# A hybrid conformer / mLSTM block on one core: heads' output turned on VectorE, tokens loaded first, start pinned, transposes mid-step, FFN entry rearranged

## The chip, the core and the metric

One of the eight cores of a Trainium2 chip. The time is that of one execution on the device, in microseconds (us); of a kernel's runs the median is given. The engines have their own instruction queues, which run in the order written: TensorE (PE: products, transposes, always into PSUM), VectorE (DVE), ScalarE (ACT), GpSimd (POOL) and SyncE (SP, which here only issues DMAs; POOL issues some too). An instruction waits at the head of its queue until the semaphores that it names have come, and all behind it wait with it.

## The reference

One layer of a diffusion backbone over 512 latent tokens (`x`, width 1024) and 256 context tokens (`ctx`), in float32:

```python
h  = rmsnorm(x) * (1 + sc1(c)) + sh1(c)          # ctx likewise, from c_ctx
p  = h @ w_in                                    # parts: glu, q, k, v, p5, gates, ab
A  = silu(layernorm(dwconv31(p0 * sigmoid(p1)))) @ w_conv_out
hm = mLSTM(q, k, v, gates)                       # 4 heads of 512, both directions
B  = (rmsnorm_per_head(hm) * m_norm_g * sigmoid(p5)) @ w_m_out
y  = sigmoid(p7) * A + sigmoid(p8) * B
x  = x + ga1 * (y @ w_out)
x  = x + ga2 * (relu((rmsnorm(x)*(1+sc2)+sh2) @ w1)**2 @ w2)
out = rmsnorm(x) * final_g
```

The six vectors sh1 ... ga2 are products of silu(c) with a 1024 x 6144 matrix and a bias.

## The kernel before, in words

Nearly every matrix product is made of three, of a rounded high part and a remainder: a weight tile `wraw` (128 x 1024) is loaded by SP, ACT casts it to `whi` (L99), DVE takes the rest as `wlo` (L100), and `mm3` (L103) multiplies hi x hi, hi x lo, lo x hi. So each weight tile costs one DMA, one ACT and one DVE instruction. `split` (L108) does the same for activations. Buffers come from pools: three of `wraw`, four each of `whi` and `wlo`, and the PSUM banks in two groups of four ("a", "b"). The order on each engine is set by a scheduler from the program's order, priorities and buffers; `issue_after` ties one instruction behind another.

Stages, with the times of the profiled execution:

- **Start (0 to 63 us).** The row c is spread over the partitions by a product and put through silu (`crow`, cL). `modload` (L189) loads the two wm tiles of one 128-channel step j, `moddot` (L197) multiplies them with cL and sums along the row, on DVE; small operations add the bias. Four token tiles xt are loaded; `xnorm` (L181) squares them on ACT with a running sum, takes 1/sqrt on POOL (`rstd_`) and scales the tile on DVE (L185). For each of eight steps j, `hmake` (L208) transposes the four tiles' 128 columns on PE (pt), applies scale and shift on ACT (hf) and splits into hT; six products of three (sacc, 18 matmuls) follow.
- **Gates (125 to 165 us).** 64 rows of gate logits go through scans on DVE; `finish` (L300) transposes Z on PE into the bank pz, and DVE copies it to zm (L305). The bank is used again by the products of p5, shown as p.
- **Heads (to 790 us).** Per head: k and q tiles with a 5-tap convolution, scores, four blocks of weights, v, and then per token tile t eighteen products into po. ACT sums the squares of po, POOL takes 1/sqrt, DVE makes hm (L555). `store` (L538), one tile late, makes four PE transposes into th, four ACT scalings with the norm's gain into st (L544, one buffer), and one DMA to hd (L546) in runs of 128 tokens (512 bytes). A 31-tap convolution (ca, L372) fills DVE at low priority. `lnfinish` (L397) stores mean and 1/sigma of the LayerNorm to lnd.
- **Branches (to 970 us).** The statistics are loaded back (lnr), normalised branch tiles and the heads' output (`hmload`, L692: load, cast, split) are multiplied with w_conv_out and w_m_out (pym). 32 more modulation tiles wmt come over POOL's queue, two ahead, and `mod` (L649) takes one dot at a time on DVE.
- **Output projection to FFN (970 to 1019 us).** The last three eighths of y @ w_out are done tile by tile (`last_part`, L788); then per token tile the residual add on DVE (L797), squares on ACT (L799), 1/sqrt on POOL, scale and shift on DVE (xh, L808 and L810), eight transposes on PE (pt), cast and split into h2T. `ff1(0)` runs in two halves of 256 tokens, `row` (L704) turns ga2 into a row on all partitions: PE transpose, ACT copy, DMA out (rowd), DMA back.
- **FFN (to the end).** Eight groups: `ff1`, `w2load` (scales w2 by ga2 on DVE, L862, casts, splits), `ff2`.

## Time and profile before

| | |
|---|---|
| median of 3 runs | 1356.4 us (1356.16 to 1357.19) |
| the profiled execution | 1357.05 us, span 1355.3, mean granted clock 0.995 |
| PE busy | 1324.4 us (98%), 6266 matmuls |
| DVE / ACT / POOL busy | 936.7 / 602.5 / 68.9 us |
| DMA | 176.36 MB in 65205 packets, 6594 of them under 512 bytes |

PE is busy nearly all the time, so the table's 98% says little of where time can be won; the list of what PE waited for and the windows by stage do. Matmuls are pipelined: the recorded length of one (0.39 us for 512 columns) is longer than the distance between the starts of two, which is the time that one more of them costs.

### The profile page before, as it was taken

The numbers are of one execution on the slowest core, as the hardware profiler recorded it, in microseconds if no ns is written. First come the engines' busy times: TensorE is split into PE (matmuls) and PEld (weight loads), VectorE is DVE, ScalarE is ACT, GpSimd is POOL, SyncE is SP. The second block draws the span as 40 slices with busy tenths as digits, with TensorE's granted clock in tenths as the row PEclk, the third lists the DMA queues.
The fourth block names the chain that finished last, engine by engine and source line by source line (L and its number), as shares of the span: only waits on it lengthen the run. The fifth ranks groups of instructions, "written<-read, shape, count | busy, mean of one in ns | idle before, by whom it ended". The sixth has DMA issues, their size and how long they took to land.

```text
span 1355.3 us, 16676 instructions
## 1 busy us (share of the span) xinstructions
PE 1324.4 (98%) x6266; PEld 1104.1 (81%) x6266; DVE 936.7 (69%) x1457; ACT 602.5 (44%) x912; POOL 68.9 (5%) x231
## 2 busy tenths in 40 slices
PE   5999999999999999999999999999999999999997
PEld 3788788888888888888888878888798888888885
DVE  5789978489674896748995477766684454554535
ACT  4548664346533465344635274322354323342223
POOL 2000100000000000000000000100000000000001
PEclk9999999999999999999999999999989999999999
DMA  9793233223332233322334479765633322333202
GB/s 329 288 334 110 89 112 105 62 63 101 104 94 67 64 100 107 96 63 66 106 96 127 124 249 312 262 189 200 219 106 96 97 92 63 123 109 109 73 22 78
DMA packets 65205, 176.36 MB, mean 130 GB/s; under 512 B 6594, under 2 KB 19042, under 8 KB 65124
## 3 DMA queue, kind: packets, MB, share of 16 engines
q1 hardware_dynamic: 60516, 158.51, 36.0%
q0 software_dynamic: 4608, 16.78, 3.9%
q8 instruction: 49, 0.80, 0.2%
q14 instruction: 32, 0.26, 0.1%
HBM read 162.99 MB, written 12.27 MB: 129 GB/s over the span
## 4 chain that ended last, share of the span: by engine, by line
PE 88%; DVE 4%; ACT 2%; DMA 2%; issue 1%; POOL 1%; SPq 0%; POOLq 0%; ACTq 0%; DVEq 0%
PE pf L104 8%; PE pf L105 8%; PE pf L106 8%; PE pv L105 3%; PE pv L104 3%; PE pv L106 3%; PE pym L106 2%; PE pym L105 2%; PE pym L104 2%; PE p L104 2%; PE p L106 2%; PE p L105 2%; PE pq L106 2%; PE pq L104 2%; PE pq L105 2%; PE pg L104 2%
## 5 line engine op out<-in xcount | busy, mean ns | idle before, releaser
L99 ACT CAST whi<-wraw 128x1024 fp32r<-128x1024 f32 (+1 forms) x159 | 164.9, 1040 | 305.7 <-PE pv L106 74.6
L100 DVE TENSOR_TENSOR wlo<-wraw,whi 128x1024 fp32r<-128x1024 f32 (+1 forms) x159 | 191.6, 1206 | 87.9 <-ACT whi L99 87.4
L372 DVE SCALAR_TENSOR_TENSOR ca<-up,col,ca 128x512 f32<-128x512 f32 x240 | 179.5, 748 | 5.7 <-ACT ca L370 0.9
L332 DVE SCALAR_TENSOR_TENSOR cacc<-craw,col,cacc 128x512 f32<-128x512 f32 (+1 forms) x128 | 110.7, 876 | 0.0
L864 ACT CAST w2h<-w2raw 128x1024 fp32r<-128x1024 f32 x32 | 32.3, 1052 | 156.3 <-PE pf L106 124.8
L105 PE MATMUL pf<-w2l,fT 128*128 128x512 f32 x256 | 99.6, 390 | 0.0
L104 PE MATMUL pf<-w2h,fT 128*128 128x512 f32 x256 | 99.2, 390 | 0.2 <-ACT w2h L864 0.2
L106 PE MATMUL pf<-w2h,fT 128*128 128x512 f32 x256 | 99.5, 389 | 0.0
L884 DVE TENSOR_TENSOR x<-pf,x 128x512 f32<-128x512 f32 x64 | 44.0, 689 | 65.8 <-PE pf L106 65.7
L104 PE MATMUL pf<-h2T,whi 128*128 128x512 f32 x224 | 87.1, 389 | 0.0
L105 PE MATMUL pf<-h2T,whi 128*128 128x512 f32 x224 | 87.1, 389 | 0.0
L106 PE MATMUL pf<-h2T,wlo 128*128 128x512 f32 x224 | 87.1, 389 | 0.0
L104 PE MATMUL pv<-whi,hT 128*128 128x512 f32 x192 | 75.4, 393 | 0.0
L106 PE MATMUL pv<-whi,hT 128*128 128x512 f32 x192 | 74.7, 389 | 0.0
L105 PE MATMUL pv<-wlo,hT 128*128 128x512 f32 x192 | 74.7, 389 | 0.0
L862 DVE TENSOR_TENSOR w2raw<-w2raw,ga 128x1024 f32<-128x1024 f32 x32 | 39.2, 1225 | 47.5 <-DMA w2raw<-in_w 46.4
L104 PEld LDWEIGHTS pf<-w2h,fT 128*128 128x128 f32 x256 | 48.0, 188 | 10.7 <-ACT w2h L864 0.7
L105 PEld LDWEIGHTS pf<-w2l,fT 128*128 128x128 f32 x256 | 48.1, 188 | 10.6 <-DVE w2l L869 0.7
L106 PEld LDWEIGHTS pf<-w2h,fT 128*128 128x128 f32 x256 | 48.1, 188 | 9.8
L104 PE MATMUL p<-whi,hT 128*128 128x512 f32 x128 | 50.8, 397 | 2.2 <-DVE zm L305 2.2
L869 DVE TENSOR_TENSOR w2l<-w2raw,w2h 128x512 fp32r<-128x512 f32 x64 | 40.7, 686 | 15.0 <-ACT w2h L864 15.0
L104 PE MATMUL pg<-hT,whi 128*128 128x512 f32 x128 | 50.6, 395 | 0.0
(354 smaller groups left out, 3344.1 us busy)
## 6 DMA issues: line engine op xcount, KB each, us to landing
wm<-in_wmt SPq DMA_DIRECT2D x32, 512.0 KB, 6.0
wmt<-in_wmt POOLq DMA_DIRECT2D x32, 512.0 KB, 4.7
wraw<-in_wqk SPq DMA_DIRECT2D x32, 512.0 KB, 3.5
wraw<-in_w SPq DMA_DIRECT2D x32, 512.0 KB, 4.7
w2raw<-in_w SPq DMA_DIRECT2D x32, 512.0 KB, 3.6
wraw<-in_wglu SPq DMA_DIRECT2D x16, 512.0 KB, 3.8
wraw<-in_wp SPq DMA_DIRECT2D x16, 512.0 KB, 3.6
wraw<-in_wv SPq DMA_DIRECT2D x16, 512.0 KB, 3.5
```

Source lines behind the costliest of these rows:

```text
L99: nc.scalar.copy(out=hi[:, s], in_=raw[:, s])
L100: wlast[0] = nc.vector.tensor_tensor(out=lo[:, s], in0=raw[:, s], in1=hi[:, s].bitcast(F32), op=ALU.subtract)
L104: mm(dst, lhsT=l[0], rhs=r[0], start=start, stop=False)
L105: mm(dst, lhsT=l[0], rhs=r[1], start=False, stop=False)
L106: mm(dst, lhsT=l[1], rhs=r[0], start=False, stop=stop)
L332: nc.vector.scalar_tensor_tensor(out=acc[:, :n], in0=raw[:, d:d + n], scalar=ccol(wc + d), in1=acc[:, :n], op0=ALU.mult, op1=ALU.add)
L372: nc.vector.scalar_tensor_tensor(out=accv, in0=up[:, :, d:d + 64], scalar=w_, in1=accv, op0=ALU.mult, op1=ALU.add)
L862: nc.vector.tensor_tensor(out=raw, in0=raw, in1=ga2, op=ALU.mult)
L864: nc.scalar.copy(out=hi, in_=raw)
L869: nc.vector.tensor_tensor(out=l_, in0=raw[:, nn], in1=hi[:, nn].bitcast(F32), op=ALU.subtract)
L884: nc.vector.tensor_tensor(out=x1[t][:, nn], in0=pf, in1=x1[t][:, nn], op=ALU.add)
```

## The change

1. **Start.** The four xt tiles are loaded ahead of col and the wm tiles. Squares of tiles 1 and 3 go to DVE. DVE scales only the first 384 columns of each tile up front; ACT scales the other 640 during step 0. Squares, scalings, dots and splits up to step 1 are tied into a fixed order on ACT, DVE and PE (`pin`). Weights, modulation and transposes of step j+1 are issued inside step j, the transposes between its two halves of products.
2. **zm** is copied from its bank by ACT instead of DVE.
3. **LayerNorm statistics** stay in two on-chip tiles (lns); the round trip through lnd goes.
4. **Heads' output.** `store` runs at once, not a tile late: DVE transposes hm in blocks of 32 x 32 into st, and four DMAs put the blocks in place, in runs of 32 tokens (128 bytes). The gain is applied in `hmload`.
5. **Output projection to FFN.** The remaining modulation dots move behind the h2T splits (`mod(tlast[0])` in `w1load`). Squares are written into the used PSUM bank. Scaling, transposing and casting of a tile (`scaled`, `turned`) are issued in a written order: tile 0 is turned ahead of the last tile's products, tile 1 behind them, tiles 2 and 3 ahead of the second half of `ff1(0)` (`rest`).
6. **ga2** is made into a row behind the last product of `ff1(0)`, not ahead of its first.

The diff, cut:

```diff
+        def pin(e, f):
+            if e in pins:
+                with tc.issue_after(pins[e].ins):
+                    pins[e] = f()
+            else:
+                pins[e] = f()
+            return pins[e]
...
-            nc.vector.tensor_scalar(out=xt, in0=xt, scalar1=rs[:, t:t + 1], scalar2=None, op0=ALU.mult)
+        def xscale(t, xt, n):
+            return nc.vector.tensor_scalar(out=xt[:, :n], in0=xt[:, :n], scalar1=rs[:, t:t + 1], scalar2=None,
+                                           op0=ALU.mult)
...
-        raw0 = modload(0, (1,))
+            hi, lo = hT[j][:, 0, o:o + n], hT[j][:, 1, o:o + n]
+            p("act", lambda: nc.scalar.activation(out=hf[:, :n], in_=pt[:, :n], func=AF.Identity,
+                                                  scale=m1[:, c, j, 1:2], bias=m1[:, c, j, 0:1]))
+            p("act", lambda: nc.scalar.copy(out=hi, in_=hf[:, :n]))
+            p("dve", lambda: nc.vector.tensor_tensor(out=lo, in0=hf[:, :n], in1=hi.bitcast(F32), op=ALU.subtract))
         xl = [xload(t + 2) for t in range(NT)]
-        raw0 |= modload(0, (0,))
+        nc.sync.dma_start(out=col, in_=a["col"])
+        raw0 = modload(0)
         for t in range(NT):
-            xnorm(t + 2, xl[t])
+            xstat(t + 2, xl[t], t % 2 == 1)
+        for t in range(NT - 1):
+            pin("dve", lambda: xscale(t + 2, xl[t], 3 * P))
+        pin("dve", lambda: moddot1(0, 0, cL, raw0[1], 1))
+        pin("dve", lambda: xscale(NT + 1, xl[NT - 1], 3 * P))
+        pin("dve", lambda: moddot1(0, 0, cL, raw0[0], 0))
+        pin("dve", lambda: modaff(0, 0))
...
+        wn = wpiece(a["was"][0], (NS, P), pin=pin)
+        hmake(0, 0, bank("pt"), xl, C, pin)
         for j in range(KT):
-            w = wpiece(a["was"][j], (NS, P))
-            moddot(j, 0, cL, raw0 if j == 0 else None)
-            hmake(j, 0, bank("pt"), xl, C)
-            for i in range(NS):
-                mm3(sacc[i], (w[0][:, i, :], w[1][:, i, :]), hsl(j, C, T), j == 0, j == KT - 1)
+            w = wn
+            if j < KT - 1:
+                wn = wpiece(a["was"][j + 1], (NS, P), pin=off if j else pin)
+                moddot(j + 1, 0, cL)
+            if j == 0:
+                xrest(0)
+                xrest(1)
+            products(j, w, range(0, NS // 2))
+            if j < KT - 1:
+                hmake(j + 1, 0, bank("pt"), xl, C, (lambda e, f: pin(e, f) if e == "pe" else f()) if j else pin)
+            if j == 0:
+                xrest(2)
+                xrest(3)
+            products(j, w, range(NS // 2, NS))
...
-                    nc.vector.tensor_copy(out=zm.rearrange("p a b -> p (a b)"), in_=pz)
+                    nc.scalar.copy(out=zm.rearrange("p a b -> p (a b)"), in_=pz)
...
-            nc.sync.dma_start(out=lnd[0], in_=mu)
-            nc.sync.dma_start(out=lnd[1], in_=rv)
...
-                th = bank_a("th")
+                st = he.tile([P, HD], F32, tag="st", name="st")
+                nc.vector.transpose(out=st, in_=hm)
                 for i in range(4):
-                    nc.tensor.transpose(th[:, i * P:(i + 1) * P], hm[:, i * P:(i + 1) * P], ident)
-                st = he.tile([P, 4, P], F32, tag="st", name="st")
-                for i in range(4):
-                    nc.scalar.activation(out=st[:, i, :], in_=th[:, i * P:(i + 1) * P], func=AF.Copy,
-                                         scale=ccol(O_MG + 4 * h + i))
-                nc.sync.dma_start(out=hd[4 * h:4 * h + 4, :, t * P:(t + 1) * P].rearrange("i p t -> p i t"), in_=st)
+                    nc.sync.dma_start(
+                        out=hd[4 * h:4 * h + 4, :, t * P + 32 * i:t * P + 32 * i + 32].rearrange(
+                            "k (b r) c -> r (k b) c", r=32),
+                        in_=st[32 * i:32 * i + 32, :].rearrange("r (b c) -> r b c", c=32))
...
-            split(hm_[k][:, 0, :], hm_[k][:, 1, :], raw)
+            nc.scalar.activation(out=hm_[k][:, 0, :], in_=raw, func=AF.Copy, scale=ccol(O_MG + k))
+            nc.vector.scalar_tensor_tensor(out=hm_[k][:, 1, :], in0=raw, scalar=ccol(O_MG + k),
+                                           in1=hm_[k][:, 0, :].bitcast(F32), op0=ALU.mult, op1=ALU.subtract)
...
-        while mraw:
-            mod()
...
+                nc.scalar.activation(out=po[2 * t + n], in_=x1[t][:, nn], func=AF.Square, scale=1.0 / 32.0,
+                                     accum_out=sqs[t][:, n:n + 1])
...
+        last_part(0)
+        scaled(0, 0)
+        scaled(0, 1)
+        last_part(1)
+        scaled(1, 0)
+        turned(0, last_part(2))
+        scaled(1, 1)
+        l3 = last_part(3)
+        scaled(2, 0)
+        turned(1, l3)
+        def rest(after):
+            scaled(2, 1)
+            scaled(3, 0)
+            turned(2, after)
+            scaled(3, 1)
+            turned(3, after)
...
+                mod(tlast[0])
...
+                if o:
+                    rest(mlast[0])
...
+            if g == 0:
+                ga2 = row(modc[:, 5, :], m1p.tile([P, D], F32, tag="r2", name="ga2"), m_)
```

Where it moves instructions, at the places that the prediction speaks of. **The start on DVE.** First rows of DVE's queue before (L201 is a dot with a wm tile, L185 the scaling of a whole token tile, xt_126 the first; L203 and L205 are small operations on the modulation m):

```order
L201 SCALAR_TENSOR_TENSOR wm,m_123<-wm,cL 128x1024
L203 TENSOR_SCALAR m_123<-m_123,col 128x1
L205 TENSOR_SCALAR m_123<-m_123,col 128x1
L185 TENSOR_SCALAR xt_126<-xt_126,rs 128x1024
L185 TENSOR_SCALAR xt_128<-xt_128,rs 128x1024
L185 TENSOR_SCALAR xt_130<-xt_130,rs 128x1024
L201 SCALAR_TENSOR_TENSOR wm,m_123<-wm,cL 128x1024
L185 TENSOR_SCALAR xt_132<-xt_132,rs 128x1024
L203 TENSOR_SCALAR m_123<-m_123,col 128x1
L100 TENSOR_TENSOR wlo<-wraw,whi 128x768 x2
L110 TENSOR_TENSOR hT_82<-hf,hT_82 128x512
```

And now (L197 squares, L204 scales 384 columns, L218 is the dot, xt_124 the first token tile):

```order
L197 SCALAR_TENSOR_TENSOR junk,ssq<-xt_126 128x1024
L197 SCALAR_TENSOR_TENSOR junk,ssq<-xt_130 128x1024
L204 TENSOR_SCALAR xt_124<-xt_124,rs 128x384
L204 TENSOR_SCALAR xt_126<-xt_126,rs 128x384
L204 TENSOR_SCALAR xt_128<-xt_128,rs 128x384
L218 SCALAR_TENSOR_TENSOR wm,m_123<-wm,cL 128x1024
L204 TENSOR_SCALAR xt_130<-xt_130,rs 128x384
L218 SCALAR_TENSOR_TENSOR wm,m_123<-wm,cL 128x1024
L229 TENSOR_SCALAR m_123<-m_123,col 128x1 x2
L231 TENSOR_SCALAR m_123<-m_123,col 128x1
L101 TENSOR_TENSOR wlo<-wraw,whi 128x768
L243 TENSOR_TENSOR hT_83<-hf,hT_83 128x512
```

Both squares and all scalings now stand ahead of the second dot, and of each tile only 384 columns are scaled here; the first split of a token tile (hT) is the twelfth row instead of the eleventh, behind one weight split instead of two.

**The gates on ACT.** ACT's queue before, around the copy of the last k tile (craw from pl) and the first use of zm (E):

```order
L320 COPY craw<-pk 128x256
L99 CAST whi<-wraw 128x1024
L321 COPY craw<-pl 128x512
L330 ACTIVATE cacc<-craw,col 128x770
L489 ACT_TABLE_LOAD
L489 ACTIVATE E_1641<-E_1641,zm 128x384
```

And now:

```order
L379 COPY craw<-pk 128x256
L100 CAST whi<-wraw 128x1024
L380 COPY craw<-pl 128x512
L364 COPY zm<-pz 128x512
L389 ACTIVATE cacc<-craw,col 128x770
L546 ACT_TABLE_LOAD
L546 ACTIVATE E_1644<-E_1644,zm 128x384
```

The copy of pz stands right behind the copy of pl. In DVE's queue it stood between convolution steps.

**The heads' output on SP.** SP's queue at the end of head 0 before (hd<-st is a tile's store, in_wqk are weight tiles of the next head's k and q):

```order
L96 DMA wraw<-in_wqk 128x1024
L546 DMA hd<-st 128x4x128 x3
L96 DMA wraw<-in_wqk 128x1024 x3
L96 DMA wraw<-in_wp 128x1024 x3
L546 DMA hd<-st 128x4x128
L96 DMA wraw<-in_wp 128x1024
```

And now:

```order
L97 DMA wraw<-in_wqk 128x1024
L598 DMA hd<-st 32x16x32 x8
L97 DMA wraw<-in_wqk 128x1024
L598 DMA hd<-st 32x16x32 x4
L97 DMA wraw<-in_wqk 128x1024
L598 DMA hd<-st 32x16x32 x4
L97 DMA wraw<-in_wqk 128x1024
```

Sixteen small stores in place of four; the weight loads that stood behind three stores now stand between them.

**The FFN's entry on DVE.** DVE's queue from the last projection products on before (L797 residual add, L808 and L810 scale and shift into xh, pt and h2T the split of a turned tile):

```order
L808 SCALAR_TENSOR_TENSOR xh<-x_7866,ss,aff_7874 128x512 x2
L810 TENSOR_TENSOR xh<-xh,sh_7882 128x512 x2
L797 TENSOR_TENSOR x_7868<-pwo,x_7868 128x512
L797 TENSOR_TENSOR x_7870<-pwo,x_7870 128x512
L110 TENSOR_TENSOR h2T<-pt_8140,h2T 128x4x128
L110 TENSOR_TENSOR h2T<-pt_8150,h2T 128x4x128
L808 SCALAR_TENSOR_TENSOR xh<-x_7868,ss,aff_7874 128x512 x2
L810 TENSOR_TENSOR xh<-xh,sh_7882 128x512 x2
L797 TENSOR_TENSOR x_7870<-pwo,x_7870 128x512
L797 TENSOR_TENSOR x_7872<-pwo,x_7872 128x512
```

And now, from the fourth tile's first add (L843 add, L852 and L854 scale and shift):

```order
L843 TENSOR_TENSOR x_7789<-pwo,x_7789 128x512
L852 SCALAR_TENSOR_TENSOR xh<-x_7787,ss_8020,aff_7791 128x512
L854 TENSOR_TENSOR xh<-xh,sh_7799 128x512
L843 TENSOR_TENSOR x_7789<-pwo,x_7789 128x512
L852 SCALAR_TENSOR_TENSOR xh<-x_7787,ss_8020,aff_7791 128x512
L101 TENSOR_TENSOR wlo<-wraw,whi 128x1024
L112 TENSOR_TENSOR h2T<-pt_8147,h2T 128x4x128
L112 TENSOR_TENSOR h2T<-pt_8154,h2T 128x4x128
L854 TENSOR_TENSOR xh<-xh,sh_7799 128x512
```

Tile 1's splits (pt_8147, pt_8154) stand behind both adds of tile 3, scalings of tile 2 and a weight split. Before, tile 0's splits (pt_8140, pt_8150) stood behind the first add of tile 2, and tile 1's scaling followed them.

More of the change, by code (lines that the diff above doesn't have):

```diff
@@ L59, in block @@
     col = cst.tile([P, NCOL], F32, name="col")
-    nc.sync.dma_start(out=col, in_=a["col"])
     ident = cst.tile([P, P], F32, name="ident")
@@ L71, in block @@
     zm = cst.tile([P, 8, 64], F32, name="zm")
+    lns = [cst.tile([P, T], F32, name=f"lns{i}") for i in range(2)]
     def ccol(o, n=1):
@@ L208, in hmake @@
-        def hmake(j, c, pt, tl, o):
+            return nc.vector.tensor_scalar(out=m1[:, c, j, 1:2], in0=m1[:, c, j, 1:2], scalar1=1.0,
+                                           scalar2=ccol(O_G1 + j), op0=ALU.add, op1=ALU.mult)
+        def hmake(j, c, pt, tl, o, p=lambda e, f: f()):
             n = len(tl) * P
             for i, xt in enumerate(tl):
-                nc.tensor.transpose(pt[:, i * P:(i + 1) * P], xt[:, j * P:(j + 1) * P], ident)
+                p("pe", lambda: nc.tensor.transpose(pt[:, i * P:(i + 1) * P], xt[:, j * P:(j + 1) * P], ident))
@@ new lines, in block, with products @@
+        for t in range(NT - 1):
[4 more added lines that the diff above has]
+        pin("dve", lambda: modaff(0, 0))
+        sacc = [(bank_a if i < 4 else bank)("sacc") for i in range(NS)]
+        off = lambda e, f: f()
+        def products(j, w, rng):
+            for i in rng:
+                mm3(sacc[i], (w[0][:, i, :], w[1][:, i, :]), hsl(j, C, T), j == 0, j == KT - 1)
+            pins["pe"] = mlast[0]
@@ new lines, in last_part, with scaled, turned @@
+            rstd2(sqs[t])
+            return mlast[0]
+        def scaled(t, hf):
+            hh = slice(hf * 512, (hf + 1) * 512)
+            xh = xhs[t, hf] = t2("xh")
+            nc.vector.scalar_tensor_tensor(out=xh, in0=x1[t][:, hh], scalar=sqs[t][:, 3:4], in1=aff2[:, hh],
+                                           op0=ALU.mult, op1=ALU.mult)
+            nc.vector.tensor_tensor(out=xh, in0=xh, in1=sh2[:, hh], op=ALU.add)
+        def turned(t, after):
+            tt = slice(t * P, (t + 1) * P)
+            for hf in range(2):
@@ L811, in block @@
                 pt = bank_a("pt2")
-                for k in range(4):
-                    nc.tensor.transpose(pt[:, k * P:(k + 1) * P], xh[:, k * P:(k + 1) * P], ident)
+                with tc.issue_after(after.ins):
+                    for k in range(4):
+                        nc.tensor.transpose(pt[:, k * P:(k + 1) * P], xhs[t, hf][:, k * P:(k + 1) * P], ident)
                 ptv = pt.rearrange("p (k t) -> p k t", k=4)
                 kk = slice(4 * hf, 4 * hf + 4)
-                split(h2T[:, 0, kk, tt], h2T[:, 1, kk, tt], ptv)
+                tlast[0] = split(h2T[:, 0, kk, tt], h2T[:, 1, kk, tt], ptv)
@@ L819, in block @@
+        last_part(0)
[14 more added lines that the diff above has]
+            turned(3, after)
         NG = 8
-        ga2 = row(modc[:, 5, :], m1p.tile([P, D], F32, tag="r2", name="ga2"))
         fg = m3p.tile([P, D], F32, tag="r1", name="fg")
```

111 lines of the change are left out of this document (51 added, 60 removed).

## The prediction

> **What bounds the kernel now.** First the page's line of engines.
>
> ```profile
> span 1355.3 us, 16676 instructions
> PE 1324.4 (98%) x6266; PEld 1104.1 (81%) x6266; DVE 936.7 (69%) x1457; ACT 602.5 (44%) x912; POOL 68.9 (5%) x231
> ```
>
> TensorE (PE) is busy for 1324.4 of 1355.3 us. The end moves only if PE gets fewer instructions, or if its 31 idle us, and what follows from them, shrink. The waits of PE say where it idles.
>
> ```profile
> PE pt L211 <- DVE xt L185: 9.6, 4, 3.6
> PE pcr L168 <- DMA cL<-in_c: 3.7, 1, 3.7
> PE pt L813 <- DVE xh L810: 2.9, 1, 2.9
> PE sacc L104 <- ACT hT L109: 2.4, 2, 2.1
> PE p L104 <- DVE zm L305: 2.2, 1, 2.2
> ```
>
> So: the start (pt, sacc), the gates (zm) and the stage between output projection and FFN (xh). The windows by stage give VectorE's (DVE's) load there, the granted clock (third number from the right) and the DMA share.
>
> ```profile
> 0.00:21.00 21.00, 5.64 (x8) 1.88 (x8) 7.33 (x13) 9.92 (x15) 6.86 (x27) 1.00 0.93 347
> 21.00:58.50 37.50, 36.32 (x158) 28.24 (x158) 31.10 (x66) 17.27 (x26) 3.10 (x4) 1.00 0.88 317
> 58.50:125.00 66.50, 66.35 (x319) 55.16 (x320) 60.81 (x111) 40.34 (x64) 1.85 (x9) 1.00 0.72 245
> 125.00:165.00 40.00, 37.78 (x204) 32.15 (x204) 38.74 (x43) 28.02 (x38) 2.78 (x12) 0.99 0.29 88
> ```
>
> Until 21 us the DMA engines are the full resource (0.93); from 58.5 to 165 DVE is busy for 99.6 of 106.5 us, so it has little room to catch up there. The profiled execution took 1357.05 us, its span and 1.75 us around it, 0.65 us above the median of the runs shown (1356.4). The sum is made against 1357.05 and brought to the median at the end.
>
> **The heads' output.** PE loses 64 transposes, in 16 groups of four; ScalarE (ACT) loses 64 scalings. Two groups in PE's timeline, with the 18 products of one tile between them (start, length, engine, line):
>
> ```profile
> 254.62 0.60 PE L541 MATMUL th<-ident,hm 128*128 128x128 f32 x4
> ...
> 257.83 0.39 PE L104 MATMUL po<-vhi,pth 128*128 128x512 f32 x1
> ...
> 259.19 0.60 PE L541 MATMUL th<-ident,hm 128*128 128x128 f32 x4
> ```
>
> The last six products take 259.19 - 257.83 = 1.36, or 0.227 us from start to start. The cycle takes 259.19 - 254.62 = 4.57, of which 18 x 0.227 = 4.08 are products; a group costs the 0.49 that is left. PE is full there, so 16 x 0.49 = 7.8 us go. The fourth group of the last head also waited:
>
> ```profile
> 790.36 0.40 PE L106 MATMUL pab<-hT,wlo 128*128 128x512 f32 x1
> 791.45 0.33 PE L541 MATMUL th<-ident,hm 128*128 128x128 f32 x1 [0.70 <-DVE hm L555]
> ```
>
> 1.09 us from start to start less 0.23 is 0.86 that goes too. Together 8.7.
>
> In their place stand 16 DVE transposes of 128x512 f32, which the trace does not have, and 64 stores of 128-byte runs. The rows nearest to both:
>
> ```profile
> L201 DVE SCALAR_TENSOR_TENSOR wm<-wm,cL 128x1024 f32<-128x1024 f32 x16 | 19.4, 1217 | 8.1 <-ACT cL L169 8.1
> ...
> L110 DVE TENSOR_TENSOR hmT<-hraw,hmT 128x512 fp32r<-128x512 f32 x16 | 10.7, 688 | 5.5 <-ACT hmT L109 5.4
> ```
>
> ```profile
> L546 SPq DMA_DIRECT2D hd<-st x16: 359/377/382, 256.6 to 794.4; - x16
> ...
> DMA to landing us min/median/max: 2.3/2.3/3.7
> ```
>
> I take 0.69 us for a transpose (same width), 1.22 (twice the width) as the other end: 11 to 20 us of DVE in all, spread over heads in which DVE waits for PE while the po products run. [...] A tile's four stores cost the SP queue 4 x 0.38 = 1.5 us to issue and some 2.3 to land, so tile t's buffer st (one only) is free about 4 us behind its transpose. Products of a tile take 18 x 0.227 = 4.1 us, but the new order puts the second transpose behind the third tile's hm, and the third behind a weight split, so 5 to 8 us lie between transposes: the wait for st is 0 to 1 us on DVE, and PE has four banks to go on in. On SP the stores now stand between weight loads of the next head, which are three buffers ahead. Cost 0; if the cover goes, see the third rival. Nothing is paid for the gain's new place: the scaling is folded into the cast and the split that hmload has anyway.
>
> **The start.** The four x tiles now come ahead of col and the first wm, two squares move to DVE, and only 384 columns are scaled before the first transposes. Two 512 KB loads of wmt that GpSimd's queue issued at the very start come behind the first rs; they are used first some 700 us later, so nobody waits for them. While DMA is full at 347 GB/s, 1.05 MB less ahead of the first product is worth about 3 us; the chain behind the last load (two dots of 1.22, a scaling, three small operations, transposes, hf, hT) is what it was, less half of each scaling. I take 2.7, with 1 to 4 as ends: the first product at 18.3 instead of 21.0. Then seven steps took 21.0 to 58.5, 5.36 us each, for a PE content of 18 x 0.227 + 4 x 0.12 = 4.6. DVE's groups in that stretch:
>
> ```profile
> L201 DVE SCALAR_TENSOR_TENSOR wm<-wm,cL 128x1024 f32<-128x1024 f32 x14 | 17.0, 1216 | 0.0
> L100 DVE TENSOR_TENSOR wlo<-wraw,whi 128x768 fp32r<-128x768 f32 x7 | 6.7, 951 | 1.2 <-ACT whi L99 1.1
> L110 DVE TENSOR_TENSOR hT<-hf,hT 128x512 fp32r<-128x512 f32 x7 | 4.8, 687 | 2.0 <-ACT hT L109 2.0
> L203 DVE TENSOR_SCALAR m<-m,col 128x1 f32<-128x1 f32 x14 | 2.8, 207 | 0.1
> ```
>
> 17.0 + 6.7 + 4.8 + 2.8 = 31.3, and 7 x 0.21 more of such small operations: 32.8, or 4.7 per step, nearly what PE needs. With everything for the next step issued half a step ahead, I estimate a pace of 4.85, a little over the longer of the two: 7 x (5.36 - 4.85) = 3.6, at most 7 x (5.36 - 4.6) = 5.3. Of 2.7 + 3.6 = 6.3 I keep 4.5, since DVE has 7 us of room up to 165 us and as many dots, splits and taps to do ahead of the gates as before. The other 640 columns of each tile are scaled on ACT between its casts; ACT is busy for 17.3 of 37.5 us there, so that is hidden. Ends: 1 and 8.
>
> **The zm copy** goes from DVE to ACT.
>
> ```profile
> 160.90 0.58 ACT L321 COPY craw<-pl 128x512 f32<-128x512 f32 x1
> 161.57 0.94 ACT L330 ACTIVATE cacc<-craw,col 128x770 f32<-128x770 f32 x1
> ```
>
> ```profile
> 161.57 1.02 DVE L332 SCALAR_TENSOR_TENSOR cacc<-craw,col,cacc 128x770 f32<-128x770 f32 x1
> 162.50 0.69 DVE L305 COPY zm<-pz 128x512 f32<-128x512 f32 x1
> ```
>
> On DVE it starts at 162.50; on ACT it stands right behind the 0.58 copy, so it can run from 161.5: 1.0 us off PE's wait. Behind this gap the clock halves:
>
> ```profile
> 163.90:167.30 3.40, 3.40 (x10) 2.62 (x9) 3.40 (x5) 3.37 (x5) 2.30 (x3) 0.50 0.02 7
> 983.10:989.90 6.80, 5.88 (x18) 5.03 (x19) 5.63 (x10) 2.52 (x6) 0.86 (x2) 0.50 0.14 55
> ```
>
> 3.4 us at 0.50 cost 1.7. Whether 1.6 us of idling still brings it, nothing here shows. [...] I count 1.0, with 0 and 2.7 as ends.
>
> **The LayerNorm statistics** stay on chip: two stores and two loads of 256 KB less. No wait of PE above names them; 0.
>
> **Output projection to FFN.** Squares go into PSUM, two modulation dots leave the queue ahead of the residual, transposes are deferred, and the ga2 row moves behind ff1(0).
>
> ```profile
> 974.50 1.23 DVE L654 SCALAR_TENSOR_TENSOR wmt<-wmt,cB 128x1024 f32<-128x1024 f32 x1 [2.15 <-DMA wmt<-in_wmt]
> ```
>
> ```profile
> 970.44:994.60 24.16, 21.27 (x92) 17.33 (x90) 18.70 (x31) 8.89 (x20) 3.50 (x7) 0.86 0.46 154
> 994.60:1019.30 24.70, 24.70 (x207) 24.53 (x206) 22.66 (x31) 15.57 (x25) 0.99 (x3) 1.00 0.49 150
> ```
>
> DVE, stuck behind a dot that waited for its wmt, was late with xh: 2.9 us of PE, and the second half-clock stretch, 5.88 busy us at half speed, 2.9 more. Up to 6 of 48.9 us are there to win. But new waits come. The first FFN product needs the second tile's h2T. Its cast stands on ACT behind the squares of the fourth tile, which need DVE's add (0.69), which needs the last projection product; its split stands on DVE behind two operations (about 0.7 and 1.2). The last square and two casts at 0.6 each (the 512-wide copy on ACT took 0.58), then a split of 0.69: with the add 3 us in which PE stands ahead of the first FFN product. And all transposes of tiles 3 and 4 now come in one piece at the start of the second half, with casts and splits behind them: 2 us. With 3 us of idling a half-clock stretch can come again (0 to 3). So 6 won, 5 + 1.5 lost: 0, with -4 and +3 as ends.
>
> **The ga2 row** must travel:
>
> ```profile
> ga<-rowd SPq DMA_DIRECT2D x2, 512.0 KB, 6.7
> ```
>
> The row's store (over 1 us) and broadcast (6.7) take 8 us, then four products with ga2 and the splits of w2 on DVE, 4 x (1.22 + 1.37) = 10, beside fT splits: some 25 to 35 us after ff1(0), and ff2(0) starts 36 to 38 after the second half's start. 0; the other end is +4.
>
> Sum: 8.7 + 4.5 + 1.0 + 0 + 0 + 0 = 14.2; 1357.05 - 14.2 = 1342.85, at the median's level 1342.2.
>
> **The rivals.** First: no new wait in the FFN stage, so 6 are won there, and both early ends hold: 8.7 + 6.3 + 2.7 + 6 = 23.7, 1332.7. For it, PE has no other wait in these stages; against it, the in-order queues of ACT and DVE just followed. Second: the start's gain is given back. DVE, at 94% from 58.5 to 165, is the bound there, and PE meets it at p <- zm again, with a half clock; the FFN stage takes its worst end. 8.7 + 0.5 + 0 - 3 = 6.2, 1350.2. Against it: DVE, too, starts earlier. Third, slower: the small stores. In the DMA row of the window 250 to 270 us (40 slices of 0.5 us), a 256 KB store of head 0 in runs of 512 bytes shows as two slices at eight or nine tenths:
>
> ```profile
> DMA  0858920000000009800000008900000007900000
> ```
>
> 512 runs in 0.85 us. The new store has as many, a quarter as long, so at most 0.85 us (below it as far as the length counts), 16 per head: 14 us of a head's 150 (the four lie between 165 and 790 us). Say that a 128-byte packet took four times the price of a 512-byte one, 3.4 us per store: a head's stores would need 54 us, from 255 to 309. On SP the last three weight loads of the next head now stand between and behind them:
>
> ```profile
> 272.00 14.65 SPq L96 DMA_DIRECT2D wraw<-in_wqk  x3
> ```
>
> The last of the three was issued at 286.6 and would come 22 us late; two pieces loaded ahead cover 2 x 24 x 0.227 = 11. 11 x 3 heads = 33 lost against 14 won: 1342.2 + 33 = 1375. From 3.5 times the price on (stores until 302, 16 late, 5 lost per head) the sign turns. [...] Against the rival: DMA share 0.2 in that stretch, and no row with such a price.
>
> **How the numbers follow.** Forecast 0.62, first rival 0.13, second 0.18, third 0.07. The forecast's ends: the small terms at their good or bad ends at once would be 1333 and 1351; that they all do so is unlikely, and 1335 to 1350 leaves out most of the first rival and the third, 2 in 10. What a measurement can tell from no change here is about 0.2%, 2.7 us. Faster by more: 0.90, the forecast, the first rival and nearly all of the second; within 0.2%: 0.04, what lies between second and third; slower: 0.06.
>
> **What would show it.** Right: no th on PE, and cycles of 18 po products in 4.1 us; the first sacc near 18.3 and the eighth step's begin near 53; a wait at zm of some 1.6 us; the waits of PE naming pf <- h2T, about 3 + 2 us, in place of pt <- xh. Wrong: a PE wait on wraw or whi in the heads behind hd stores landing late, a DVE transpose over 2 us, PE's wait at zm as long as before, or a wait of ff2 on w2h of over 3 us.

## The result, and the profile after

| | before | after |
|---|---|---|
| median, same session | 1356.8 us (4 runs, 1356.2 to 1357.9) | 1367.5 us (4 runs, 1367.1 to 1369.0) |
| profiled execution | 1357.05, span 1355.3 | 1367.05, span 1365.3 |
| mean granted clock | 0.995 | 0.988 |

The changed kernel is slower: ratio 1.008, 95% interval 1.0063 to 1.0098, some 11 us where 14 fewer were forecast. First the page's line of engines, of the kernel after:

```profile
span 1365.3 us, 16552 instructions
PE 1321.0 (97%) x6202; PEld 1099.6 (81%) x6202; DVE 948.2 (69%) x1476; ACT 589.7 (43%) x850; POOL 69.5 (5%) x231
```

PE has the 64 transposes less (6202 for 6266) and is busy for 3.4 us less, but the span is 10.0 longer: what grew is PE's idle time. The waits of PE, after (in total, times, longest):

```profile
PE pc L106 <- ACT sig L723: 13.7, 1, 13.7
PE pt L237 <- DVE xt L204: 7.2, 2, 6.2
PE pf L106 <- ACT h2T L111: 4.4, 2, 3.6
PE spc L106 <- ACT khi L111: 2.8, 1, 2.8
```

Three of the four stand where before had none: pc is the first branch product (y @ w_conv_out), pf the first FFN product, spc the scores of the first head. The start's wait (pt) shrank and the one at zm is gone. Three stretches of the windows view (fields after the engines: granted clock, DMA share, GB/s) show what follows the gaps:

```profile
175.10:181.93 6.83, 6.06 (x15) 4.71 (x16) 5.14 (x8) 4.05 (x6) 0.17 (x3) 0.50 0.28 82
806.57:823.64 17.07, 5.44 (x13) 4.31 (x14) 11.39 (x19) 12.32 (x20) 0.96 (x2) 0.50 0.98 374
1001.13:1004.54 3.41, 3.25 (x16) 2.96 (x16) 3.41 (x6) 1.10 (x2) 0.96 (x2) 0.50 0.57 154
```

Each wait is followed by a stretch at half clock. Of the 17.07 us, PE was busy for 5.4, so half of that, 2.7, is lost beside the wait itself. The starts of the first products of each stage, from PE's timeline of both kernels, place the loss:

| stretch | before | after | difference | predicted |
|---|---|---|---|---|
| begin to the first po (head 0) | 246.45 | 247.08 | +0.6 | -5.5 |
| first po to first pc | 565.94 | 571.12 | +5.2 | -8.7 |
| first pc to first pwo | 130.85 | 133.50 | +2.6 | 0 |
| first pwo (output projection) to the end | 412.05 | 413.58 | +1.5 | 0 |
| sum | 1355.29 | 1365.28 | +10.0 | -14.2 |

The second row misses by 13.9, which is the wait at pc. Without it the heads would have given what was forecast: between the first po of head 0 and that of head 3 lie 517.36 us instead of 523.32, 2.0 less per head. The steps inside the heads came out too, as the groups by line, the tile view of st and PE's timeline show (the first products of two token tiles in a row, 18 products apart, no th between):

```profile
L596 DVE STREAM_TRANSPOSE st<-hm 128x512 f32<-128x512 f32 x16 | 11.2, 702 | 0.1
```

```profile
L598 SPq DMA_DIRECT2D hd<-st x64: 302/490/1564, 254.5 to 803.6; - x64
...
DMA to landing us min/median/max: 1.8/2.3/4.3
```

```profile
255.24 0.39 PE L106 MATMUL po<-vhi,pth 128*128 128x512 f32 x1
...
259.32 0.39 PE L106 MATMUL po<-vhi,pth 128*128 128x512 f32 x1
```

0.70 us for a transpose, 2.3 from issue to landing for a store in 128-byte runs (2.3 before with 512-byte runs and four times the bytes), and 4.08 us for a tile's products instead of 4.57.

What failed stands behind the heads. The branch tiles cv are normalised there: SP loads them, DVE subtracts and multiplies (L710, L711), ACT applies silu (L712) and casts them into act (L111), DVE takes the rest (L112), and ACT's four sigmoids (L723) empty the PSUM banks that pc needs. ACT's timeline, after:

```profile
787.95 1.05 ACT L100 CAST whi<-wraw 128x1024 fp32r<-128x1024 f32 x1 [4.48 <-PE pab L107]
...
803.87 1.52 ACT L712 ACTIVATE cv<-cv,col 128x512 f32<-128x512 f32 x2 [3.27 <-DVE cv L711]
805.29 1.03 ACT L100 CAST whi<-wraw 128x1024 fp32r<-128x1024 f32 x1
806.82 0.81 ACT L712 ACTIVATE cv<-cv,col 128x512 f32<-128x512 f32 x1 [0.50 <-DVE cv L711]
807.54 4.24 ACT L111 CAST act<-cv 128x512 fp32r<-128x512 f32 x8
814.24 1.95 ACT L745 ACTIVATE hmT<-hraw,col 128x512 fp32r<-128x512 f32 x3 [2.46 <-DVE act L112]
816.21 1.28 ACT L723 ACT_TABLE_LOAD   x1
817.50 2.06 ACT L723 ACTIVATE sig<-pab 128x512 f32<-128x512 f32 x4
```

and DVE's, after:

```profile
789.03 1.23 DVE L101 TENSOR_TENSOR wlo<-wraw,whi 128x1024 fp32r<-128x1024 f32 x1 [3.87 <-ACT whi L100]
790.18 1.22 DVE L699 SCALAR_TENSOR_TENSOR wmt<-wmt,cB 128x1024 f32<-128x1024 f32 x1
...
801.36 0.70 DVE L596 STREAM_TRANSPOSE st<-hm 128x512 f32<-128x512 f32 x1
801.98 1.25 DVE L710 TENSOR_TENSOR cv<-cv,lns 128x512 f32<-128x512 f32 x2
...
809.30 4.90 DVE L112 TENSOR_TENSOR act<-cv,act 128x512 fp32r<-128x512 f32 x8
```

PE's last pab product starts at 804.07. Read backwards from pc at 818.20: the sigmoids have had their operands since about 804, but stand on ACT behind three casts of the heads' output (L745), which wait for DVE's last split of act; that stands behind the last cv operations, which stand on DVE behind the last transpose of hm, weight splits (L101) and modulation dots (L699). The first of those splits (789.03) waited 3.87 us for its cast on ACT (787.95), and the cast 4.48 us until PE freed a whi buffer; from 789.03 to 814.2 DVE is never idle. So from the first cv operation to the last split of act the chain takes 22.3 us (791.95 to 814.2), 7.8 of them for other work between (weight splits, dots, a transpose). Before, it took 15.0 with no other work between, as DVE's timeline shows, and ACT had the sigmoids ahead of the casts, so that the whole chain was level with PE:

```profile
794.77 0.69 DVE L665 TENSOR_TENSOR cv<-cv,lnr 128x512 f32<-128x512 f32 x1 [3.37 <-DMA cv<-cdr]
...
805.44 4.29 DVE L110 TENSOR_TENSOR act<-cv,act 128x512 fp32r<-128x512 f32 x7
```

```profile
805.98 0.81 ACT L667 ACTIVATE cv<-cv,col 128x512 f32<-128x512 f32 x1
...
810.61 1.58 ACT L678 ACTIVATE sig<-pab 128x512 f32<-128x512 f32 x3
812.05 0.63 ACT L109 CAST hmT<-hraw 128x512 fp32r<-128x512 f32 x1
```

There PE ended pab at about 812 and found the banks empty. After, PE came 8 us earlier and the chain 7 later: 13.7 of wait.

### The profile page after: what moved, and what is told of

It is laid out like the page before. It is cut to its first block, busy times and chain, and to the rows that moved or that the text cites. A ratio compares the mean times of both kernels' runs of the same rounds, so it can differ in the third digit from the quotient of the medians.

```text
span 1365.3 us, 16552 instructions
## 1 busy us (share of the span) xinstructions
PE 1321.0 (97%) x6202; PEld 1099.6 (81%) x6202; DVE 948.2 (69%) x1476; ACT 589.7 (43%) x850; POOL 69.5 (5%) x231
## 4 chain that ended last, share of the span: by engine, by line
PE 85%; DVE 6%; ACT 3%; DMA 2%; issue 2%; POOL 1%; SPq 0%; POOLq 0%; ACTq 0%; DVEq 0%
PE pf L107 8%; PE pf L108 8%; PE pf L106 8%; PE pv L108 3%; PE pv L107 3%; PE pv L106 3%; PE pg L106 2%; PE pg L108 2%; PE pym L108 2%; PE pg L107 2%; PE pym L107 2%; PE pym L106 2%; PE pq L108 2%; PE pq L107 2%; PE pq L106 2%
## 5 line engine op out<-in xcount | busy, mean ns | idle before, releaser
L101 DVE TENSOR_TENSOR wlo<-wraw,whi 128x1024 fp32r<-128x1024 f32 (+1 forms) x159 | 191.6, 1206 | 79.4 <-ACT whi L100 78.7
L108 PE MATMUL pq<-hT,wlo 128*128 128x512 f32 x128 | 50.0, 391 | 0.7 <-DVE wlo L101 0.7
```

The source lines that it names most:

```text
L101: wlast[0] = pin("dve", lambda: nc.vector.tensor_tensor(out=lo[:, s], in0=raw[:, s], in1=hi[:, s].bitcast(F32), op=ALU.subtract))
L108: mlast[0] = mm(dst, lhsT=l[1], rhs=r[0], start=False, stop=stop)
```

## The experiments

The theory from here on: the heads' saving is real, but at pc PE meets a chain on ACT and DVE whose order the scheduler chose anew, and the FFN's entry and the start bring smaller losses. Rivals: the stores in short runs delay SP; the start alone is at fault; the sigmoids' place on ACT is the whole of it. Each session has its own runs of before; ratios are against those.

### Parts alone

**heads_only**: before, with the heads' output of the change and nothing else (edit as in the change's part 4).

```diff
-                th = bank_a("th")
+                st = he.tile([P, HD], F32, tag="st", name="st")
+                nc.vector.transpose(out=st, in_=hm)
...
-                pend = (t, hm)
+                store(t, hm)
```

> The kernel before with the heads' output alone changed (DVE transposes, four stores per tile, gain in hmload). The prediction's step: 8.7 us less, 1348. Chain or order theory: 2 us per head less up to the last head (6), then the wait at pc with its half clock: the way from the last head's first product to pc takes 53.8 us as in the changed kernel instead of 42.6, so 11 - 6 + 2.7 = 8 more than before, 1363 to 1366. If the wait at pc came from the LayerNorm statistics kept on chip, it would not show here.

It took 1362.3 us against 1355.9, ratio 1.0042 (1.0027 to 1.0057), just under what the chain theory gave it. PE's waits have the stall at the size it has in after; the profile goes by the last arrival and puts it down to a load:

```profile
PE pc L104 <- DMA sig<-sd: 13.6, 1, 13.6
```

So the heads' output alone makes the stall and a loss of 6 us, without the new start and the new entry to the FFN.

**start_zm**: before, with parts 1 and 2 only.

```diff
-                    nc.vector.tensor_copy(out=zm.rearrange("p a b -> p (a b)"), in_=pz)
+                    nc.scalar.copy(out=zm.rearrange("p a b -> p (a b)"), in_=pz)
...
+            xstat(t + 2, xl[t], t % 2 == 1)
```

> The kernel before with the start and the zm copy alone changed. The prediction's step: 5.5 us less, 1351. DVE-bound theory (DVE has the same work ahead of the last k tile, and PE meets it at the first scores, spc <- khi): the first product 3.6 us earlier, but a wait of 3 to 5 us at spc with a half-clock stretch, and the first po product within 1.5 us of the 246.4 of before: 1356 to 1358.

It took 1354.1 us against 1355.9, ratio 0.9986 (0.9976 to 0.9995): 1.8 us won where the prediction had 5.5 and the other theory nothing. PE's first product comes at 17.61 (before 21.01), the first k product of head 0 at 121.81 (122.55), the first po at 245.71 (246.45). Of 3.4 us at the start, 0.7 is left by head 0.

**sig_first**: after, with the casts of the heads' output tied behind the last sigmoid.

```diff
+            with tc.issue_after(siglast[0].ins):
+                nc.scalar.activation(out=hm_[k][:, 0, :], in_=raw, func=AF.Copy, scale=ccol(O_MG + k))
```

> The changed kernel, in which the casts of the heads' output (hmT) on ACT are tied behind the last of the four sigmoids (sig) that empty the PSUM banks for which the first branch product pc waits 13.7 us. Order theory (the casts stand in front of the sigmoids on ACT, and that is the whole wait): the wait at pc goes, and the half-clock stretch behind it: 13.7 + 2.7 less, about 1351. Chain theory (PE comes to pc 8 us earlier than before, while the LayerNorm's chain of loads, DVE operations, silu, casts ends no earlier; the order only adds to it): the last cast of act ends at 811.8, table load and sigmoid take 2, so pc starts near 813.8 instead of 818.2: 4 to 5 less, about 1363, and a wait of some 9 us stays. Store theory (the 128-byte stores hold the loads of cv back): no change, 1367.5.

It took 1362.4 us, ratio 1.0045 (1.0029 to 1.0061), as the chain theory had it. The wait falls from 13.7 to 9.3, the half-clock stretch behind it from 17.07 to 10.24. The sigmoids' place is a third of the stall; two thirds lie in the chain ahead.

**stores_big**: after, with each store one run of 2048 bytes per partition; the heads' output lands in other places than it should.

```diff
-                        out=hd[4 * h:4 * h + 4, :, t * P + 32 * i:t * P + 32 * i + 32].rearrange(
-                            "k (b r) c -> r (k b) c", r=32),
+                        out=hd[4 * h + t, 32 * i:32 * i + 32, :],
```

> The changed kernel with the same four stores per tile, but each to one contiguous place in runs of 2048 bytes, so the heads' output lands in the wrong places in memory; all instructions and waits stay. Store theory: the wait at pc (13.7 us) goes for the most part, 1353 to 1357. Order and chain theory: no change within 1.5 us, 1366 to 1369, and the wait at pc stays over 12 us.

It took 1352.3 us, ratio 0.9967 (0.9954 to 0.998), and the wait at pc falls to 1.6. The store theory had forecast nearly that (1353 to 1357), and it looks like a verdict on short runs, but it isn't one: the landing only falls from 2.3 to 1.7 us, and with the other stores the scheduler also wrote another order (transposes right behind hm, cv chain from 788 on, sigmoids ahead of the casts). Two causes changed at once; the next runs keep the 128-byte runs and change the order.

### A second buffer, and the old FFN entry

**st2** gives st a second buffer; **st2_noffn** also puts before's way into the FFN back (parts 5 and 6 undone).

```diff
-                st = he.tile([P, HD], F32, tag="st", name="st")
+                st = he.tile([P, HD], F32, tag="st", name="st", bufs=2)
```

```diff
-        last_part(0)
-        scaled(0, 0)
...
+        while mraw:
+            mod()
...
+            for n in range(2):
+                last_part(n)
+                residual(n)
```

> The changed kernel with two buffers of st instead of one, a single number; the stores keep their runs of 128 bytes. In the order that results, each DVE transpose stands right behind its hm, the last head's stores leave SP ahead of the weights and the sigmoids stand ahead of the hmT casts on ACT, as they did in the run with runs of 2048 bytes. Order theory (with one st the planner puts the transposes and so the stores, the loads of cv behind them and the LayerNorm's chain late; the runs' length itself costs nothing): the wait at pc falls from 13.7 to 2 or less, 1351 to 1354. Store theory (runs of 128 bytes themselves hold the queue or the loads): the wait at pc stays over 8 us, 1361 or more.

> As the run with two st buffers, with the way from output projection to FFN (modulation dots, squares, transposes, ga2 row) as in the kernel before. The prediction's step for that part was 0 (-4 to +3). From the first pwo product to the end the changed kernel took 413.6 us and the kernel before 412.1: the part is a loss of 1.5 to 2.5 us, so this run is 1.5 to 2.5 us faster than the one with two st buffers alone. Had the part won what it removes (the waits at xh and the half clock, 6 us), this run would be 6 us slower.

st2 took 1362.0 us, ratio 1.0033 (1.0021 to 1.0046), and st2_noffn 1357.9, ratio 1.0019 (1.0009 to 1.0028). The first misses what the order theory gave it and lies where the store theory had it. All stores and sigmoids stand where they should, yet pc still waits 9.7 us. PE's wait and DVE's timeline of st2 say why:

```profile
PE pc L106 <- issue: 9.7, 1, 9.7
```

```profile
787.78 1.23 DVE L101 TENSOR_TENSOR wlo<-wraw,whi 128x1024 fp32r<-128x1024 f32 x1 [3.11 <-ACT whi L100]
...
793.22 1.23 DVE L101 TENSOR_TENSOR wlo<-wraw,whi 128x1024 fp32r<-128x1024 f32 x1 [3.07 <-ACT whi L100]
...
795.50 0.69 DVE L710 TENSOR_TENSOR cv<-cv,lns 128x512 f32<-128x512 f32 x1
798.66 1.22 DVE L101 TENSOR_TENSOR wlo<-wraw,whi 128x1024 fp32r<-128x1024 f32 x1 [2.47 <-ACT whi L100]
799.80 0.69 DVE L711 TENSOR_TENSOR cv<-cv,lns 128x512 f32<-128x512 f32 x1
```

The weight splits for pc were put ahead of the cv operations. Their casts on ACT can't run until PE frees a buffer (every 5.4 us, at PE's pace), so the chain that PE will need next is held to PE's own pace by work for later. Undoing the FFN's entry is worth 4.1 us (1362.0 - 1357.9), more than the 1.5 to 2.5 that were expected.

**st2_taps** and **st2_taps_noffn** are the same two with 30 taps of the first 31-tap convolution tied behind the fourth k tile's split, to give DVE room ahead of head 0.

```diff
+                    if j:
+                        conv31(j, up)
+                    else:
+                        late.append(lambda: conv31(0, up))
```

> As the run with two st buffers, with the 30 taps of the first 31-tap convolution (0.75 us each on DVE) tied behind the fourth k tile's split instead of ahead of it. DVE-bound theory (the start's gain is lost because DVE has 22 us of taps ahead of what the first scores need): the wait at spc <- khi of 2.5 to 3 us and the half-clock stretch behind it go, and the first po product comes 5 to 6.5 us earlier; if the taps don't bring a new wait at pm (213 us), 5 to 6 us faster than with two st buffers alone. If the wait at spc came from ACT's zm copy or its table loads, the wait stays within 1 us of what it was.

> Both of the two edits above on the kernel with two st buffers. If they touch different stages, their effects add: about 7.5 us faster than two st buffers alone, some 1344 to 1346.

They took 1362.4 us (1.0041, 1.0026 to 1.0056) and 1357.9 (1.001, 1.0001 to 1.002), which is no gain. The wait at spc is gone, and another of 2.4 us stands 17 us further on (`PE tp <- DVE pm`): the work was put off, and PE met it there. The pair again gives 4.5 us for the FFN's entry.

### DVE ties, and the taps left out

**chain_first** (after), **chain_heads** (heads_only) and **chain_st2_noffn** (st2_noffn) tie the modulation dots and the splits of w_conv_out behind the last cv operation, on DVE alone.

```diff
-            mod()
+            mod(cvlast)
+        def behind(e, f):
+            if e == "act":
+                return f()
+            with tc.issue_after(cvlast.ins):
+                return f()
...
+            w = wpiece(a["wco"][j], (KT, P), pin=behind)
```

> The changed kernel (one st buffer) with two ties on DVE: the modulation dots and the splits of the w_conv_out weights stand behind the LayerNorm's chain on cv instead of between its operations. The run with two st buffers showed what else is in the way: its order on ACT was right and its stores were early, yet the wait at pc was 9.8 us, and on DVE the first operation on cv came at 795.5 though its data was there before 791, because weight splits stood in front that waited for a cast, which waited for PE. DVE-order theory: the chain ends near 802 instead of 806.8, the splits of act near 807 instead of 814.2, pc starts near 810: 7 to 9 us less, 1358 to 1361. If the wait hung on something else (loads of cv or sig, PSUM banks), it stays within 2 us of 13.7 and the time at 1366.

> The kernel before with the heads' output changed, and the two ties on DVE. The heads' output alone took 1362.3, with a wait of 13.6 at pc. DVE-order theory: the wait falls to 3 or less with its half clock gone, and the prediction's 8.7 us come out: 1347 to 1351. If not, it stays at 1358 or more.

> The changed kernel with two st buffers, the way into the FFN as before, and the two ties on DVE; without the ties it took 1357.9 with a wait of 9.8 at pc. DVE-order theory: the chain starts when cv is there (790) and ends near 801, the sigmoids are done near 805, PE comes to pc at 802.5: the wait falls to 3 or less and the half-clock stretch with it: 7 to 10 us less, 1348 to 1351, which is faster than both kernels.

They took 1363.9 us (1.0059, 1.004 to 1.0078), 1361.3 (1.0039, 1.0024 to 1.0054) and 1357.1 (1.0003, 0.9994 to 1.0013). All three miss their forecasts: pc still waits 12.0 in the first, 5.2 and 4.9 in two pieces in the second, and 8.7 in the third. In the third, DVE's cv operations run from 789.8 on, but ACT reaches the first silu only at 799.8, behind a cast of whi at 797.45 that waited 4.38 us for PE. One queue freed is not enough; the same work stood at the head of the other.

**taps_out**: after, with 20 of the 31 taps of the first convolution tile left out.

```diff
-                for d in range(31):
+                for d in range(31 if j else 11):
```

> The changed kernel with 20 of the 31 taps of the first convolution tile left out (20 x 0.75 = 15 us of DVE, all ahead of the first scores), so that tile's result is wrong. DVE-bound theory of the start: the wait at spc (3 us and more) and the half-clock stretch go, nothing new takes their place since the work is gone and not moved, and the first po product comes 5.5 to 6.7 us earlier (240.4 to 241.6 instead of 247.1). Rival (ACT's order with its copy of zm and table loads makes the wait): it stays, 245 or later. The wait at pc may take back what is won; the time itself says little.

It took 1362.6 us, ratio 1.0046 (1.003 to 1.0063). The windows of the start, first of after, then of taps_out (DVE is the third busy time):

```profile
58.50:125.00 66.50, 65.32 (x312) 53.30 (x311) 62.60 (x113) 41.21 (x66) 1.85 (x9) 1.00 0.74 264
125.00:165.00 40.00, 40.00 (x215) 34.16 (x215) 37.85 (x42) 26.70 (x36) 2.17 (x12) 1.00 0.33 94
```

```profile
58.50:125.00 66.50, 65.31 (x311) 53.23 (x311) 60.28 (x108) 41.29 (x65) 2.19 (x11) 1.00 0.75 266
125.00:165.00 40.00, 40.00 (x215) 34.11 (x214) 32.07 (x32) 27.68 (x39) 2.48 (x12) 1.00 0.31 94
```

With 8.1 us less on DVE in these two windows (100.45 to 92.35) the wait at spc falls from 2.8 to 0.7, no half-clock stretch follows, and the first po comes 5.0 us earlier (242.10 for 247.08). So DVE's work sets when head 0 begins. The stall at pc stays 13.7, but pc itself comes 5.0 us earlier (813.18 for 818.20) and the time falls by 4.9 (1362.6 for 1367.5). So what is won at the start is not lost at pc: the chain, whose first split waits for a cast at PE's pace, comes earlier with PE. What makes the stall is how long the chain takes from there.

### Both queues in order

The c4 kernels tie on both engines: w_conv_out's casts from the second tile on stand behind the last silu on ACT, its splits behind the last cv operation on DVE, and four modulation dots behind the last split of act.

```diff
+        def behind(e, f):
+            with tc.issue_after((lsilu if e == "act" else cvlast).ins):
+                return f()
...
+        for _ in range(4):
+            mod(alast)
...
+            w = wpiece(a["wco"][j], (KT, P), pin=lambda e, f: f() if j == 0 else behind(e, f))
```

**c4_st2_noffn** is st2_noffn with it, **c4_st2** st2, **c4_heads_st2** heads_only with two st buffers, **c4_before** the kernel before.

> The changed kernel with two st buffers, the way into the FFN as before, and the order around the LayerNorm's chain on both engines: the weights of the second and later w_conv_out tiles are cast on ACT behind the last silu of cv and split on DVE behind the last operation on cv, the first tile's stay in front, and the four modulation dots come behind the splits of act. The run with ties on DVE alone moved the chain on DVE to 789.8 to 800.8, yet ACT began its silu only at 799.8, since a weight cast in front of it waited for PE until 797.4; pc started at 811.7 after a wait of 8.7. Queue-order theory: silu follows DVE from 791 on, the sigmoids end near 805, PE comes to pc at 802.7 and waits 3 us or less, with no half clock: 7 us less than the 1357.1 with DVE's ties alone, 1348 to 1351, and faster than both kernels. If the wait at pc stays over 7 us, something else holds it (loads of sig, the banks), and the time stays at 1355 or more.

> The same with the new way into the FFN. That part cost 4 us in the pair of runs with two st buffers (1362.0 against 1357.9): 1352 to 1355 here.

> The kernel before with the heads' output alone changed, two st buffers and the same order around the LayerNorm's chain. The heads' output alone took 1362.3. Queue-order theory: the 2 us per head and the 0.9 at the last group arrive at the end at last, less a wait of up to 3 at pc: 1348 to 1351. If the heads' output itself were dear (DVE's transposes, 64 stores), it stays above 1354.

> The kernel before with that order around the LayerNorm's chain and nothing else. Queue-order theory: before, PE came to pc at 812.4 and found its operands ready, so there is nothing to win: within 2 us of the kernel before, 1354 to 1358. If the order by itself makes the kernel faster by 5 us or more, the gain in the other runs says nothing of the heads' output.

| | median (before 1356.3) | ratio | first pc |
|---|---|---|---|
| c4_st2_noffn | 1353.5 | 0.9984 (0.9972 to 0.9995) | 805.01 |
| c4_st2 | 1356.8 | 1.0002 (0.9993 to 1.0012) | 804.78 |
| c4_heads_st2 | 1355.4 | 0.9994 (0.9984 to 1.0003) | 805.43 |
| c4_before | 1359.0 | 1.0019 (1.0007 to 1.003) | 813.38 |

By medians the first is 2.8 us faster than before, by its interval 0.7 to 3.8, and so faster than both kernels. All four come out above their forecasts, by 2.5, 1.8, 4.4 and 1.0 us. The ACT timeline of c4_st2_noffn (the chain runs through, and the sigmoids start as pab ends):

```profile
801.36 1.65 ACT L111 CAST act<-cv 128x512 fp32r<-128x512 f32 x3
803.02 1.28 ACT L723 ACT_TABLE_LOAD   x1
804.32 2.07 ACT L723 ACTIVATE sig<-pab 128x512 f32<-128x512 f32 x4
806.24 1.36 ACT L749 ACTIVATE hmT<-hraw,col 128x512 fp32r<-128x512 f32 x2
```

and PE's waits at pc, first of c4_st2_noffn, then of c4_st2:

```profile
PE pc L108 <- DVE wlo L101: 3.2, 3, 1.7
...
PE pc L106 <- issue: 1.3, 1, 1.3
```

```profile
PE pc L108 <- DVE wlo L101: 2.0, 3, 1.4
...
PE pc L106 <- issue: 1.3, 1, 1.3
```

c4_st2 differs from st2 in the ties alone: pc's wait falls from 9.7 to 1.3, then 2.0 on wlo, and the ratio from 1.0033 to 1.0002. So of the 9.7 us in st2 the order on the two queues makes all but 1.3, not the stores and not PE's work. The step from 13.7 in after to 9.7 in st2 came with the second buffer and the order that went with it; no run has the ties on both queues with one buffer.

With the order put right, most of the heads' saving arrives at pc: from the first po to the first pc c4_st2_noffn takes 558.67 us, before 565.94, so 7.3 of the 8.7. But what is tied back is now late itself (wlo, 3.2 in c4_st2_noffn), and from pc to the first pwo it takes 135.08 for 130.85, so 4.2 are lost again. c4_before shows that the ties are no gain by themselves: it waits 1.1 us on wlo and is 2.7 slower by medians, though in its profiled execution 1.1 of the 1.8 longer span were there at the first po already (247.51 for 246.45).

c4_heads_st2 waits 4.8 at pc, then 2.7 on wlo, and two half-clock stretches of 3.41 us follow; its LayerNorm statistics still go out and back. c4_st2 against c4_st2_noffn gives 3.3 us for the FFN's entry once more. And stores_big, which has the same FFN entry as c4_st2, is 4.5 us faster by medians (1352.3 for 1356.8): in the profiled executions 2.9 of them lie between pc and the first pwo (130.95 for 133.89), where c4_st2 has its tied splits. Whether the longer runs have a share in the rest was not tried.

## Why the prediction was wrong, point by point

**The heads' output** (8.7, "Cost 0; if the cover goes, see the third rival"): the step that failed. Its parts held: 0.49 per tile on PE, 0.70 for the transpose, 2.3 for a store. It followed the new DVE and SP rows only as far as PE waits inside the heads ("the wait for st is 0 to 1 us on DVE, and PE has four banks to go on in"), and took it that PE's gain runs on to the end. It never asked what PE meets at the next join, nor whether the other operand comes earlier too. Measured: -2.0 per head up to the last head's po (shown by after), then 13.7 at pc and 2.6 of half clock (shown as the heads' doing by heads_only). The chain to pc had grown from 15.0 to 22.3 us (22.2 in heads_only, from 790.49 to 812.64). That the order makes the wait is shown in after itself for 4.4 of the 13.7 us by sig_first, and in st2 for 8.4 of the 9.7 by c4_st2 (ratio 1.0002 for 1.0033); for the rest of after's wait it is argued from the rows. That the LayerNorm statistics cost 0 because "no wait of PE above names them" is the same slip: a chain with no wait today has no price, but it has a slack, and here the slack was under 2 us (sigmoids from 810.61, pc at 812.39).

**The start** (4.5 + 1.0): the first product was forecast for 18.3 and came at 17.4, the eighth step for 53 and came at 53.2 (58.5 before), and zm's wait went whole. But nothing of these 5.3 us was left at the first po, +0.6. The second rival had the mechanism, DVE at 94% from 58.5 to 165 us, with the meeting place at zm; it is at spc, 172 us. taps_out shows it: less DVE work, and head 0 begins earlier. The argument "DVE, too, starts earlier" failed since DVE has 100 of 106 us to do there and no more room than before. In start_zm 0.7 us remains at the first po and 1.8 in the whole.

**Output projection to FFN** (0, -4 to +3): the two waits came where they were worked out, 3.6 us ahead of the first FFN product (forecast 3) and about 1 in the second half (forecast 2). The size was off: three pairs of kernels price the entry at 4.1, 4.5 and 3.3 us against before's way in the same surroundings, around the bad end of -4. ACT's timeline, after, shows what the count left out:

```profile
997.62 0.60 ACT L844 ACTIVATE pwo<-x 128x512 f32<-128x512 f32 x1 [0.90 <-DVE x L843]
998.16 0.19 ACT L844 ACTIVATION_READ_ACCUMULATOR pwo<-x 128x1 f32 x1
998.25 1.03 ACT L100 CAST whi<-wraw 128x1024 fp32r<-128x1024 f32 x1
999.61 0.60 ACT L844 ACTIVATE pwo<-x 128x512 f32<-128x512 f32 x1 [0.33 <-DVE x L843]
1000.14 0.19 ACT L844 ACTIVATION_READ_ACCUMULATOR pwo<-x 128x1 f32 x1
1000.23 1.05 ACT L111 CAST h2T<-pt 128x512 fp32r<-128x512 f32 x2
```

A weight cast stands among the squares, and the gap is followed by half a clock for 3.4 us. In the pair st2 and st2_noffn PE's gap, from start to start, is 3.93 and 2.61, and only the first has a half-clock stretch (3.41, so 1.7 lost): 1.3 + 1.7 + the second half's 1 make the 4. And of the 6 us that were to be won, the half clock's 2.9 don't need the new entry: st2_noffn has before's entry and no such stretch, and takes 409.8 us from the first pwo to the end, before 412.1, st2 413.5.

**The rivals.** The third, small stores, is false: landing is unchanged at 2.3 us, PE has no wait over 0.1 us between 177 and 804 us in after, and c4_st2_noffn is faster with them than before. A store in 128-byte runs lands 0.6 us later than one in 2048-byte runs (2.3 us in after, 1.7 in stores_big, both of 64 KB); what makes the difference no run shows. The first fell with its premise of no new wait. None of the three had the stall at pc, so 0.06 for slower was too little.

**Why an order does this.** In these timelines ACT and DVE work in the order written: behind one cast that waits for PE, silu and sigmoids wait with it. In chain_st2_noffn the first cv operations end at about 791, and their silu starts at 799.82, behind the cast that waited 4.38 us.

**Open.** c4_heads_st2 still waits 4.8 at pc: its first cv operation waits 4.12 us for its load until 790.58, the chain then runs through to the sigmoids at 804.74, and PE ended pab at 800.66; why the load comes no earlier was not tried. By medians c4_st2_noffn gains 2.8 us, with 0.7 to 3.8 as its interval, and its profiled execution (1351.5) is the lowest of its ten runs; a kernel that also removes the 3.2 us on wlo was not tried. Why the scheduler puts the weight splits ahead was read from its rows only.

## What to carry to other kernels

A saving on the bound engine may last only to the next place where it meets another chain: before counting it to the end, find that place, read there how long the other operand had been ready, and whether it will come earlier too or, by a new order, later. A changed buffer or engine makes a scheduler write a new order far from the edit, so compare the queues up to that join and look there for work for later that waits, at the head of the line, for the bound engine itself. And an experiment that changes a size may change the order too: read the rows before giving the size the credit.

## What the runs showed of the hardware

- In these runs many idle gaps of PE were followed by half-clock stretches of 3.41 us or a multiple (gaps are counted here from start to start of two products): 3.07 us of gap brought 6.83 in after, 14.1 brought 17.07 there. Gaps of 1.68 (start_zm) and 1.83 us (c4_st2_noffn) at 173 us brought 3.41, while one of 2.05 at 816 us and one of 2.81 at 978 us in c4_st2_noffn brought none. So what a short gap cost beside itself was not set by its length alone: nothing here, 1.7 us (half of 3.41) there.
- A 128x512 float32 transpose in 32x32 blocks took 0.70 us on DVE, about as long as an add of that width (0.69). The prediction had taken 0.69.
